# Neighbourhood attention: keys loaded once and doubled on GpSimd, shorter pattern loads, heads asked for a head earlier

## The chip, the cores and the metric

The kernel runs on one core of a Trainium2 chip. The metric is the device time of one execution in microseconds (us), as the median of several runs. A core has five instruction streams that matter here: TensorE (PE in the profile; PEld is its weight load), VectorE (DVE), ScalarE (ACT), GpSimd (POOL) and SyncE (SP), which issues most of the DMAs. Each engine works through its own stream in order and waits on semaphores for the others. A DMA runs on its own once it is issued.

## The reference

The reference is a network of two layers on 2048 tokens (a grid of 32 rows and 64 columns) and 256 context tokens, width 1024, in 32-bit floats. Layer 0 is a convolution beside full attention; layer 1 is Fourier mixing beside neighbourhood attention; each ends with a gate and an output projection. The change lies in the neighbourhood attention of layer 1, which has 8 heads of 64 channels:

```python
s_win = einsum('brqhd,brkwhd->bhrqkw', qg, kb) * scale + bias      # 8 rows of the grid around a query's row
s_win = where(col_ok, s_win, NEG_INF)                              # 16 columns around a query's column
s_ctx = einsum('brqhd,bchd->bhrqc', qg, kc) * scale                # and all 256 context tokens
p = softmax(concatenate([s_win, s_ctx]))
o = p_win @ v_window + p_ctx @ v_context
```

The bias depends on the offset between query and key, and on the head.

## The kernel before

A product of 32-bit floats is made from two rounded parts, a high and a low one (`a = 0, 1` in the code): a query's high part stands on partitions 0 to 63 and its low part on 64 to 127, and one product with 128 rows of contraction takes both against the same key part. For that the key part must stand **twice**, on partitions 0 to 63 and again on 64 to 127. `load_keys` (L1511) therefore loads each of a head's two key tiles (`nk0`, `nk1`, 128 x 2304) by two DMAs of 64 x 2304 from the same place in memory, and the queries (`nq`, 128 x 2048) by two of 64 x 2048. The tiles of a head come from `kp[h % 2]`, two pools of one buffer each: a head's keys can be loaded once the scores of the head two before it are done.

The bias and the mask are kept as patterns: for each head, nine kinds of [128 x 512], loaded as three tiles `pat0`, `pat1`, `pat2` of [128 x 3 x 768] whose first 256 columns (the context) are zero.

The work of a head is cut into four **units** (t = 0 to 3, 16 columns of the grid each), and a unit's scores into four **chunks** (i = 0 to 3, a band of rows). A chunk is this chain over the engines:

- TensorE: four products into one PSUM tile `ns`, two over the 256 context keys (L1577, a = 0 and 1), two over the window's 384 or 512 keys (L1581).
- DVE: `evict` (L1589) adds the pattern and takes the least value; later a reciprocal of the sum (L1603).
- ACT: the exponential (L1596).
- POOL: `normalise` (L1604), [128 x 640] or [128 x 768].

When a unit's four chunks are normalised, six jobs follow it: transposes on TensorE (`npt`, L1635), the split into high and low on ACT (`nhi`, L1640) and DVE (`nlo`, L1642), and products with the values (`nav`, L1655 and L1656). After the last, ACT copies the sum to `ny2`, a DMA moves half of it to other partitions (`ny3`, L1670), and POOL adds the two into the output `yd` (L1673). Values come by `load_values` (L1540): four DMAs of `nv` for each unit (L1549), one of `nvc` for each head (L1544).

What sets the order: `stream` (L1734) writes the order of TensorE, DVE, ACT and POOL by hand. It goes through the units (i = 0 to 31) and their six jobs (j = 0 to 5); the scores run two units and two chunks ahead of the jobs. In each step `extra(i, j)` may add work of its own. SyncE's order is not written out: a scheduler places its DMAs by what they wait for, except those of the first units that are put into the program's order by `keep_in_program_order`. SyncE works through its queue in order, with eight places for DMAs in flight; a DMA that finds its place taken, or its buffer not free, holds all behind it.

Just ahead of the stage the Fourier mixing ends: its last transforms (L1406 to L1408, L1456 to L1458) are on TensorE, its last results are stored by DMAs from ACT's queue (L1477, four of 1 MB).

Of the kernel before, what the change touches and what calls it, by code (L numbers as in the profile page):

```python
# [20 lines left out]
P = 128  # L21
# [28 lines left out]
def dft_tables():  # L50
    """Cosines and sines of 512 rows for the even and the odd frequencies, and those of a channel group."""
# [9 lines left out]
class Stream:  # L61
    """What is due on each engine in the coming steps."""
# [21 lines left out]
class Build:  # L84
# [132 lines left out]
    def adaln(self, layer, j, raw, psum, mo, brow=None):  # L217
        """256 columns of the shift, scale and gate of one layer: in four steps.

        Four column tiles hold sums over a quarter of the rows each, for both conditions.  # L220
        """
# [161 lines left out]
    def load_w(self, raw_of, wp, w, n0, scale=1.0, eng=None, hold=None, load=True):  # L383
        """High and low parts of 256 columns of a weight, as two halves of its rows."""
# [22 lines left out]
    def mm_channel(self, ps, w, h, c, cols, ks=range(KT)):  # L407
        """ps[128 channels, tokens] from weight columns c*128.. and a block's columns."""
# [25 lines left out]
    def ab_proj(self):  # L434
# [5 lines left out]
        with ExitStack() as es:  # L440
# [134 lines left out]
            def ada_tiles():  # L575
                """Where the modulation's weights wait, 256 columns at a time: in tiles that nothing else needs yet."""
# [191 lines left out]
    def load_kv(self):  # L768
        """Keys as [high; high] and as [low; four rows of ones], and values."""
# [19 lines left out]
    def ab_attention(self):  # L789
        """Scores with the keys on partitions, shifted by each query's greatest score.  # L790

        A unit is two heads of one group for 256 queries. Its greatest scores come from products of one pass, with
        the queries on partitions, a unit ahead; they are rounded and go into the scores as four more rows of the
        contraction, one for each 128 queries.
        """
        nc = self.nc
        with ExitStack() as es:
# [56 lines left out]
            def chunk(i, qt, c):  # L854
                """Part of the least (negated) score of 128 queries."""
# [54 lines left out]
            def add(i, k):  # L910
                """Sums over the keys: one on DVE, one on Pool."""
# [32 lines left out]
            def total(i):  # L944
                """A row of sums, which DMAs put on 128 partitions for the reciprocals, and copy to all for the products."""
# [123 lines left out]
    def load_wout_part(self, raw, w, k, n, eng):  # L1069
        """One block of the rows of half of an output projection's columns."""  # L1070
        ins = self.nc.sync.dma_start(raw, w[k * P : (k + 1) * P, n * 512 : n * 512 + 512])
        if n == 0:
            self.tc.keep_in_program_order(ins)
        yield 1
        hi, lo = self.wout[2 * n : 2 * n + 2]
        self.split(hi[:, k], lo[:, k], raw, eng)
# [15 lines left out]
    def out_norm(self, psum, b):  # L1092
        """Layer norm and SiLU of the convolution of 256 tokens."""
# [58 lines left out]
    def out_gate(self, b):  # L1152
        """Gates 256 tokens of both branches and splits them."""
# [182 lines left out]
    # Rows n and 2048-n, then n and 1024-n, are folded together, so that 512 rows are left for the even and for  # L1336
    # the odd frequencies of the cosine and of the sine part; row 512 is added as a vector of signs.
    def fourier_early(self, psum):
        """What is ready before the last input projections are: channel tables, a table, the first two groups."""
# [24 lines left out]
    def fold(self, g, gp, psum):  # L1364
        """A group's folded rows after the channel transform, with rows on partitions."""
# [48 lines left out]
    def dft_table(self, q, rp):  # L1414
        """A quarter of the table of the sequence transform, split."""
# [458 lines left out]
```

## Time and profile before

| what | value |
|---|---|
| median of 3 runs (lowest, highest) | 2954.23 us (2945.24, 2960.78) |
| span of the profiled execution, first to last instruction | 2944.6 us |
| what the median lies above that span | 9.6 us |
| mean granted TensorE clock | 0.970 |
| busy: PE, DVE, POOL, ACT | 94%, 63%, 52%, 39% |
| the stage of the change | 2405 to 2758 us of the span |
| moved by DMA from 2405 to 2745 us | 77.89 MB, 229 GB/s |

The page lists no time of its own for the profiled execution, only its span, so the span stands for it. PE's busy share is an average over the whole program: in most of it the large projections and the attention of layer 0 keep TensorE busy. Busy times of a stage are read in windows of that stage. "Clock" is the share of full speed that was granted to TensorE; it falls for some microseconds after TensorE was idle. A row "X <- Y" among the waits says that X was idle until Y was done.

### The profile page before, as it was taken

Reading aid. Unit: us, or ns where it says so; the run is one execution under the profiler, and the core shown is the slowest. Engines: PE = TensorE matmul, PEld = TensorE weight load, DVE = VectorE, ACT = ScalarE, POOL = GpSimd, SP = SyncE. Lnnn points to the kernel's source line nnn. Section 1 sums busy time; section 2 is a strip of 40 time slices with the busy share of each in tenths; the row PEclk is TensorE's granted clock in tenths of the full one; section 3 lists DMA queues with packets and bytes.
Section 4 is the critical chain, followed back from the end, with each engine's and each line's share of the span. In section 5 each row is a group of like instructions: output and inputs, shape, how many; then the busy total and the mean of one; then the engine's idle time right before and its main releaser. Section 6 shows DMA issues by size and latency. Waiting matters only on the chain.

```text
span 2944.6 us, 40977 instructions
## 1 busy us (share of the span) xinstructions
PE 2764.9 (94%) x14481; PEld 2128.3 (72%) x14481; DVE 1855.9 (63%) x2867; ACT 1134.3 (39%) x2103; POOL 1531.5 (52%) x1173
## 2 busy tenths in 40 slices
PE   7988799986999999999999999999999997998998
PEld 5988799886444444444445887988898886888787
DVE  4798869896877788888887564101211336777663
ACT  3223131320354555555554223123222335777421
POOL 3568624846465788778785754222122312455343
PEclk9999899998999999999999999999999998999999
DMA  8224131361642343331123653433333349999852
GB/s 249 91 77 147 53 106 47 96 179 36 196 136 78 123 138 101 90 121 55 51 63 106 235 166 136 150 127 106 126 140 128 111 152 238 220 246 225 273 197 89
DMA packets 345752, 397.66 MB, mean 135 GB/s; under 512 B 54844, under 2 KB 270444, under 8 KB 340555
## 3 DMA queue, kind: packets, MB, share of 16 engines
q1 hardware_dynamic: 344971, 390.85, 44.9%
q10 hardware_dynamic: 576, 4.19, 0.4%
q8 instruction: 114, 1.87, 0.3%
q14 instruction: 91, 0.75, 0.1%
HBM read 270.34 MB, written 129.78 MB: 136 GB/s over the span
## 4 chain that ended last, share of the span: by engine, by line
PE 65%; DMA 11%; DVE 9%; POOL 6%; issue 4%; ACT 1%; SPq 0%; POOLq 0%; ACTq 0%; DVEq 0%
PE av L900 9%; PE s L885 9%; PE mm L415 7%; PE mm L417 7%; PE mm L416 7%; PE m L862 6%; DVE acc L517 5%; DMA nv<-v_d 4%; POOL wlo L431 4%; PE mo L1087 3%; PE mo L1086 3%; PE mo L1085 3%; DMA nk<-k 3%; PE mm L424 2%; PE mm L426 1%
## 5 line engine op out<-in xcount | busy, mean ns | idle before, releaser
L431 POOL TENSOR_TENSOR wlo<-wraw,whi 128x1024 fp32r<-128x1024 f32 x86 | 323.8, 3774 | 499.7 <-ACT whi L430 481.1
L864 DVE TENSOR_REDUCE ast<-m 128x1 f32<-128x512 f32 (+1 forms) x656 | 398.7, 626 | 176.8 <-PE m L862 174.5
L890 ACT ACTIVATE pr<-s 128x512 f32<-128x512 f32 x584 | 343.1, 595 | 298.6 <-PE s L885 253.9
L925 POOL TENSOR_TENSOR accp<-accp,pr 128x512 f32<-128x512 f32 x283 | 398.7, 1409 | 88.1 <-ACT pr L890 74.2
L517 DVE SCALAR_TENSOR_TENSOR acc<-u,cw,acc 128x1151 f32<-128x1151 f32 (+1 forms) x240 | 366.5, 1582 | 0.0
L900 PE MATMUL av<-pr,vt 128*64 128x512 f32 x1168 | 317.4, 622 | 0.0
L417 PE MATMUL mm<-hi_ab,wlo 128*128 128x384 f32 x768 | 260.6, 341 | 39.1 <-POOL wlo L431 39.1
L415 PE MATMUL mm<-hi_ab,whi 128*128 128x384 f32 x768 | 261.0, 346 | 11.6 <-DVE qraw L729 7.2
L416 PE MATMUL mm<-lo_ab,whi 128*128 128x384 f32 x768 | 261.7, 342 | 0.0
L415 PE MATMUL mm<-hi_cd,whi 128*128 128x512 f32 x640 | 250.8, 392 | 1.1 <-ACT hi_cd L379 1.1
L416 PE MATMUL mm<-lo_cd,whi 128*128 128x512 f32 x640 | 250.1, 391 | 0.4 <-DVE lo_cd L380 0.4
L417 PE MATMUL mm<-hi_cd,wlo 128*128 128x512 f32 x640 | 246.7, 390 | 0.0
L417 PEld LDWEIGHTS mm<-hi_ab,wlo 128*128 128x128 f32 x768 | 147.5, 192 | 39.8 <-POOL wlo L431 39.8
L925 DVE TENSOR_TENSOR accd<-accd,pr 128x512 f32<-128x512 f32 x165 | 165.7, 1004 | 0.9 <-ACT pr L890 0.5
L1642 DVE TENSOR_TENSOR nlo<-npt,nhi 128x512 fp32r<-128x512 f32 x192 | 123.6, 644 | 62.1 <-ACT nhi L1640 61.4
L862 PEld LDWEIGHTS m<-k1h,q 128*128 128x128 f32 x328 | 62.2, 190 | 132.9 <-DVE ast L864 84.9
L415 PEld LDWEIGHTS mm<-hi_ab,whi 128*128 128x128 f32 x768 | 147.5, 193 | 14.1 <-DVE qraw L729 7.6
L1604 POOL TENSOR_SCALAR npr<-npr,nst 128x640 f32<-128x640 f32 (+1 forms) x128 | 108.1, 858 | 89.8 <-DVE nst L1603 66.7
L371 DVE TENSOR_SCALAR ht<-ptr,scale,shift 128x384 f32<-128x384 f32 (+2 forms) x96 | 61.2, 671 | 147.4 <-PE ptr L368 146.7
L862 PEld LDWEIGHTS m<-k0h,q 128*128 128x128 f32 x328 | 63.3, 195 | 125.0 <-DVE ast L864 80.6
L430 ACT ACTIVATE whi<-wraw 128x1024 fp32r<-128x1024 f32 x88 | 92.9, 1059 | 148.3 <-PE mm L416 135.5
L416 PEld LDWEIGHTS mm<-lo_ab,whi 128*128 128x128 f32 x768 | 147.8, 193 | 0.8 <-DVE lo_ab L380 0.8
(321 smaller groups left out, 7002.1 us busy)
## 6 DMA issues: line engine op xcount, KB each, us to landing
wraw<-in_cd_w_in_dram SPq DMA_DIRECT2D x46, 512.0 KB, 4.0
wraw<-in_ab_w_in_dram SPq DMA_DIRECT2D x42, 512.0 KB, 3.5
pat_d<-big SPq DMA_DIRECT2D x72, 256.0 KB, 3.7
nk<-k SPq DMA_DIRECT2D x32, 576.0 KB, 12.7
pat<-pat_d SPq DMA_DIRECT2D x24, 768.0 KB, 6.5
nv<-v_d SPq DMA_DIRECT2D x128, 128.0 KB, 7.0
adaraw<-in_ab_w_ada_dram SPq DMA_DIRECT2D x24, 512.0 KB, 6.1
adaraw<-in_cd_w_ada_dram SPq DMA_DIRECT2D x24, 512.0 KB, 3.7
```

What stands on the lines that cost most here:

```text
L415: nc.tensor.matmul(ps, a, hh[:, k, cols], start=k == 0, stop=False)
L416: nc.tensor.matmul(ps, a, hl[:, k, cols], start=False, stop=False)
L417: nc.tensor.matmul(ps, b, hh[:, k, cols], start=False, stop=k == KT - 1)
L431: (eng or nc.vector).tensor_tensor(out=lo, in0=src, in1=hi.bitcast(F32), op=ALU.subtract)
L517: ins = nc.vector.scalar_tensor_tensor(out=acc[:, :n], in0=u[:, tap : tap + n], scalar=cw[:, ch, tap : tap + 1], in1=acc[:, :n], op0=ALU.m ...
L862: nc.tensor.matmul(ps[:, :n], lhs, kt[hp // 2][0][:, a : a + n], start=True, stop=True)
L864: nc.vector.tensor_reduce(out=s["st"][:, qt, col : col + 1], in_=ps[:, :n], axis=AX.X, op=ALU.min)
L885: nc.tensor.matmul(ps[:], kt[hp // 2][key][:, k * P : k * P + P], s[x][:].rearrange("p j n -> p (j n)"), start=key == 0, stop=key == 1,)
L890: nc.scalar.activation(pr[:], ps[:], AF.Exp, scale=-1.0)
L900: nc.tensor.matmul(s["av"][x * 64 : x * 64 + 64], vt[:, k - 1 + x, kv * 64 : kv * 64 + 64], s["pr"][k - 1 + x][:], start=k == 1, stop=k == ...
L925: eng.tensor_tensor(out=s[name][:], in0=first_in[:], in1=s["pr"][k][:], op=ALU.add)
L1642: return lambda: nc.vector.tensor_tensor(out=lo[:, :o], in0=pt[:, :o], in1=hi[:, :o].bitcast(F32), op=ALU.subtract)
```

## The change

Four things, all in `natten`:

- For heads 1 to 7 each key tile is loaded once, to partitions 0 to 63; GpSimd then copies it to 64 to 127 in six pieces of 384 columns (`double`), twelve for a head. Head 0 is loaded twice as before (`whole`).
- The copies for head h + 1 are issued one in each step while the jobs of head h's units 0 and 1 run (`extra`).
- A pattern tile is loaded by two DMAs, one of [128 x 2 x 384] for the first and the last kind, one of [128 x 512] for the middle one, so that the columns 384 to 511 of the first and last kind, which no chunk reads, are left out.
- The keys and queries of head h + 1 are asked for where those of head h were asked for (of head 1: one unit later), four units ahead. Only head 0's are put into the program's order.

```diff
+            def load_head(h, whole):
+                m, r0 = h // 2, (h % 2) * 64
+                qt = kp[h % 2].tile([P, S], F32R, name="nq", tag="nq")
+                ks = [kp[h % 2].tile([P, T], F32R, name=f"nk{a}", tag=f"nk{a}") for a in range(2)]
+                heads[h] = (qt, ks)
+                for a in range(2):
+                    load(whole, ks[a][0:64].bitcast(F32), self.k2_d[m][a, r0 : r0 + 64])
+                    if whole:
+                        load(whole, ks[a][64:128].bitcast(F32), self.k2_d[m][a, r0 : r0 + 64])
+                for a in range(2):
+                    load(whole, qt[64 * a : 64 * a + 64].bitcast(F32), self.q2_d[m][a, r0 : r0 + 64])
+
+            PIECE = T // 6
+
+            def double(h, x):
+                a, i = divmod(x, 6)
+                k = heads[h][1][a]
+                cols = slice(i * PIECE, i * PIECE + PIECE)
+                nc.gpsimd.tensor_copy(k[64:128, cols], k[0:64, cols])
...
             def load_keys(u):
                 h, t = u
                 first = u in units[:5]
...
-                if t == 0:
-                    qt = kp[h % 2].tile([P, S], F32R, name="nq", tag="nq")
-                    load(qt[0:64].bitcast(F32), self.q2_d[m][0, r0 : r0 + 64])
-                    load(qt[64:128].bitcast(F32), self.q2_d[m][1, r0 : r0 + 64])
-                    ks = []
-                    for a in range(2):
-                        k = kp[h % 2].tile([P, T], F32R, name=f"nk{a}", tag=f"nk{a}")
-                        for r in range(2):
-                            load(k[r * 64 : r * 64 + 64].bitcast(F32), self.k2_d[m][a, r0 : r0 + 64])
-                        ks.append(k)
-                    heads[h] = (qt, ks)
+                if u == units[0]:
+                    load_head(0, True)
                 if t != 2:
                     kind = kind_of[t]
-                    load(
-                        pats[kind][:, :, 256:768],
-                        self.pat_d[:, h].rearrange("(r k) p c -> k p r c", k=3)[kind],
-                    )
+                    pat = self.pat_d[:, h].rearrange("(r k) p c -> k p r c", k=3)[kind]
+                    load(first, pats[kind][:, ::2, 256:640], pat[:, ::2, 0:384])
+                    load(first, pats[kind][:, 1, 256:768], pat[:, 1])
+                if t == (h == 0) and h + 1 < HEADS:
+                    load_head(h + 1, False)
...
+                if i % 4 < 2 and i // 4 + 1 < HEADS:
+                    double(i // 4 + 1, 6 * (i % 4) + j)
```

The order of TensorE, DVE and ACT stays as it was, row by row. SyncE's queue and POOL's change; three places show how. The first is SyncE at the start of the stage. Before, from the first load on (`nk0_21811`, `nk1_21814` and `nq_21808` are head 0's, `nvc_22294` is head 1's):

```order
L1544 DMA nvc_22294<-v2_d_120 128x2x128 [waits DMAHW0_49,DVE_49]
L1517 DMA nq_21808<-q2_0_112 64x2048 [waits DMAHW2_49,PE_49]
L1517 DMA nq_21808<-q2_0_112 64x2048 [waits DMAHW3_49]
L1517 DMA nk0_21811<-k2_0_116 64x2304 [waits DMAHW4_49,PE_49]
L1517 DMA nk0_21811<-k2_0_116 64x2304 [waits DMAHW5_49]
L1517 DMA nk1_21814<-k2_0_116 64x2304 [waits DVE_49,DMAHW6_49,PE_49,Pool_49]
L1517 DMA nk1_21814<-k2_0_116 64x2304 [waits DMAHW7_49]
L1517 DMA pat0_21800<-pat_d_132 128x3x512 [waits DMAHW0_49,PE_49]
```

And with the change (`nk0_21822`, `nk1_21823` and `nq_21821` are head 1's, `nk0_21809`, `nk1_21810` and `nq_21808` head 0's):

```order
L1513 DMA nk0_21822<-k2_0_116 64x2304 [waits DMAHW0_49,DVE_49,DMAHW4_49,PE_49,Pool_49]
L1513 DMA nk1_21823<-k2_0_116 64x2304
L1513 DMA nq_21821<-q2_0_112 64x2048 [waits DMAHW2_49]
L1513 DMA nq_21821<-q2_0_112 64x2048 [waits DMAHW3_49]
L1556 DMA nvc_22316<-v2_d_120 128x2x128
L1513 DMA nk0_21809<-k2_0_116 64x2304 [waits DMAHW6_49]
L1513 DMA nk0_21809<-k2_0_116 64x2304 [waits DMAHW7_49]
L1513 DMA nk1_21810<-k2_0_116 64x2304 [waits DMAHW0_49,DVE_49]
L1513 DMA nk1_21810<-k2_0_116 64x2304 [waits DMAHW1_49]
L1513 DMA nq_21808<-q2_0_112 64x2048 [waits DMAHW2_49]
L1513 DMA nq_21808<-q2_0_112 64x2048 [waits DMAHW3_49]
L1513 DMA pat0_21800<-pat_d_132 128x2x384 [waits DMAHW4_49,PE_49]
```

Head 1's loads now stand ahead of head 0's, and the first of them carries the wait on PE, DVE and POOL that stood at head 0's second key. (Before, head 1's stood behind the patterns and the first values.) For the later heads the key loads keep their place between values and patterns, two rows less.

The second place is POOL at the border between two heads, here ahead of head 2. Before, the last unit of head 1:

```order
L1673 TENSOR_TENSOR yd_22151<-ny2_22408,ny3_22409 64x32x16 [waits DMAHW5_49]
L1604 TENSOR_SCALAR npr_22510<-npr_22510,nst_22516 128x640 [waits PE_49,DVE_49,Activation_49,Pool_49]
L1604 TENSOR_SCALAR npr_22534<-npr_22534,nst_22540 128x768 [waits PE_49,DVE_49,Activation_49,Pool_49]
L1604 TENSOR_SCALAR npr_22574<-npr_22574,nst_22580 128x768 [waits DVE_49,PE_49,Activation_49]
L1604 TENSOR_SCALAR npr_22599<-npr_22599,nst_22605 128x640 [waits PE_49,DVE_49,Activation_49,Pool_49]
```

With the change, the same five rows (`nk1_22006` is head 2's; its copies are those numbered 6 to 11):

```order
L1537 COPY nk1_22006<-nk1_22006 64x384 [waits DMAHW1_49,DMAHW5_49,DMAHW0_49,Pool_49]
L1537 COPY nk1_22006<-nk1_22006 64x384
L1685 TENSOR_TENSOR yd_22171<-ny2_22431,ny3_22432 64x32x16 [waits DMAHW0_49]
L1616 TENSOR_SCALAR npr_22535<-npr_22535,nst_22541 128x640 [waits PE_49,DVE_49,Activation_49,Pool_49]
L1537 COPY nk1_22006<-nk1_22006 64x384 [waits Pool_49]
L1616 TENSOR_SCALAR npr_22560<-npr_22560,nst_22566 128x768 [waits PE_49,DVE_49,Activation_49,Pool_49]
L1537 COPY nk1_22006<-nk1_22006 64x384 [waits Pool_49]
L1537 COPY nk1_22006<-nk1_22006 64x384
L1616 TENSOR_SCALAR npr_22602<-npr_22602,nst_22608 128x768 [waits PE_49,DVE_49,Activation_49,Pool_49]
L1537 COPY nk1_22006<-nk1_22006 64x384 [waits Pool_49]
L1616 TENSOR_SCALAR npr_22628<-npr_22628,nst_22634 128x640 [waits PE_49,DVE_49,Activation_49,Pool_49]
```

Six copies stand among that unit's normalisations, behind the addition; six more among those of the unit ahead.

The third place is TensorE at the first chunk of head 2, with the change:

```order
L1589 MATMUL ns_22671<-nk0_22005,nq_22004 128x256 [waits DVE_49,DMAHW7_49,PE_49,Pool_49]
L1589 MATMUL ns_22671<-nk1_22006,nq_22004 128x256 [waits Pool_49]
L1593 MATMUL ns_22671<-nk0_22005,nq_22004 128x384
L1593 MATMUL ns_22671<-nk1_22006,nq_22004 128x384 [waits Pool_49]
L1667 MATMUL nav_22609<-nhi_22557,nv_22318 128x256
```

The rows and their order are those of before, but three of the four products now wait for POOL; the last reads columns that copies 6 to 8 write. Behind them stand the products of an older unit with its values.

More of the change, by code (lines that the diff above doesn't have):

```diff
@@ L1510, in natten, with load @@
             heads, vals, ctxs, probs, youts, left = {}, {}, {}, {}, {}, {}
+            def load(first, dst, src):
+                ins = nc.sync.dma_start(dst, src)
+                if first:
+                    self.tc.keep_in_program_order(ins)
+            def load_head(h, whole):
[15 more added lines that the diff above has]
+                nc.gpsimd.tensor_copy(k[64:128, cols], k[0:64, cols])
             def load_keys(u):
@@ L1514, in load_keys @@
                 first = u in units[:5]
-                def load(dst, src):
-                    ins = nc.sync.dma_start(dst, src)
-                    if first:
-                        self.tc.keep_in_program_order(ins)
-                m, r0 = h // 2, (h % 2) * 64
-                if t == 0:
-                    qt = kp[h % 2].tile([P, S], F32R, name="nq", tag="nq")
-                    load(qt[0:64].bitcast(F32), self.q2_d[m][0, r0 : r0 + 64])
-                    load(qt[64:128].bitcast(F32), self.q2_d[m][1, r0 : r0 + 64])
-                    ks = []
-                    for a in range(2):
-                        k = kp[h % 2].tile([P, T], F32R, name=f"nk{a}", tag=f"nk{a}")
-                        for r in range(2):
-                            load(k[r * 64 : r * 64 + 64].bitcast(F32), self.k2_d[m][a, r0 : r0 + 64])
-                        ks.append(k)
-                    heads[h] = (qt, ks)
+                if u == units[0]:
+                    load_head(0, True)
                 if t != 2:
                     kind = kind_of[t]
-                    load(
-                        pats[kind][:, :, 256:768],
-                        self.pat_d[:, h].rearrange("(r k) p c -> k p r c", k=3)[kind],
-                    )
+                    pat = self.pat_d[:, h].rearrange("(r k) p c -> k p r c", k=3)[kind]
[3 more added lines that the diff above has]
+                    load_head(h + 1, False)
             def load_values(u):
```

## The prediction

> **What bounds the kernel now.** I read the page first (its opening line, the chain, the DMA issues), then a table of windows over the neighbourhood attention, then the waits of that stage, and at last the timelines of TensorE, GpSimd and SyncE around the places that the change touches. The change lies in one stage, so the shares of the whole span only say where to look:
>
> ```profile
> span 2944.6 us, 40977 instructions
> ...
> PE 65%; DMA 11%; DVE 9%; POOL 6%; issue 4%; ACT 1%; SPq 0%; POOLq 0%; ACTq 0%; DVEq 0%
> ...
> nk<-k SPq DMA_DIRECT2D x32, 576.0 KB, 12.7
> pat<-pat_d SPq DMA_DIRECT2D x24, 768.0 KB, 6.5
> nv<-v_d SPq DMA_DIRECT2D x128, 128.0 KB, 7.0
> ```
>
> The three issue rows are all of this stage: 18.9 MB of keys, 18.9 MB of patterns, 16.8 MB of values. Windows of the stage (columns: length, busy time of PE, PEld, DVE, ACT, POOL with counts, granted clock, DMA share, GB/s):
>
> ```profile
> 2412.00:2440.00 28.00, 27.21 (x142) 23.02 (x141) 9.23 (x18) 6.75 (x14) 4.68 (x5) 1.00 0.87 233
> 2440.00:2470.00 30.00, 19.66 (x111) 14.34 (x111) 21.25 (x58) 19.15 (x41) 11.90 (x14) 0.89 1.06 255
> ...
> 2440.00:2710.00 270.00, 230.17 (x1553) 211.07 (x1554) 198.20 (x502) 192.39 (x411) 123.29 (x135) 0.91 1.05 237
> 2710.00:2740.00 30.00, 29.26 (x219) 27.11 (x218) 26.30 (x67) 27.26 (x60) 17.22 (x20) 1.00 0.58 172
> ```
>
> For 270 us the DMA engines are full (share 1.05 at 237 GB/s) while TensorE is not and runs at clock 0.91. Once the last loads are done, TensorE is full at clock 1.00. So two limits lie close together: transfers until 2710, TensorE after. The waits of the stage (total, times, longest) and the gaps name the transfers:
>
> ```profile
> PE nav L1655 <- DMA nv<-v_d: 25.5, 6, 7.6
> PE ns L1577 <- DMA nk<-k: 8.9, 2, 4.5
> ...
> 2449.40 0.38 PE L1635 MATMUL npt<-ident,npr 128*128 128x128 f32 x2
> ...
> 2465.51 0.55 PE L1577 MATMUL ns<-nk,nq 128*128 128x256 f32 x1 [4.32 <-DMA nk<-k]
> ...
> 2514.37 0.48 PE L1577 MATMUL ns<-nk,nq 128*128 128x256 f32 x2
> ...
> 2691.82 0.35 PE L1655 MATMUL nav<-nhi,nv 128*128 128x256 f32 x1 [2.57 <-DMA nv<-v_d]
> ...
> 2703.02 0.48 PE L1577 MATMUL ns<-nk,nq 128*128 128x256 f32 x2
> ...
> 2731.78 0.48 PE L1577 MATMUL ns<-nk,nq 128*128 128x256 f32 x2
> ```
>
> 2449.40 is the first transpose of the loop; 2514.37 and 2703.02 are the first scores of heads 2 and 7, five heads apart, so a head takes 37.7 us; 2731.78 is the last chunk of scores. GpSimd shows what a unit takes when nothing is late:
>
> ```profile
> 2700.58 1.69 POOL L1604 TENSOR_SCALAR npr<-npr,nst 128x768 f32<-128x768 f32 x2 [1.30 <-DVE nst L1603]
> 2702.35 1.29 POOL L1673 TENSOR_TENSOR yd<-ny,ny 64x512 f32<-64x512 f32 x1
> 2704.22 1.68 POOL L1604 TENSOR_SCALAR npr<-npr,nst 128x640 f32<-128x640 f32 x2 [0.59 <-DVE nst L1603]
> 2708.35 1.69 POOL L1604 TENSOR_SCALAR npr<-npr,nst 128x768 f32<-128x768 f32 x2 [2.44 <-DVE nst L1603]
> 2710.12 1.29 POOL L1673 TENSOR_TENSOR yd<-ny,ny 64x512 f32<-64x512 f32 x1
> 2712.01 1.69 POOL L1604 TENSOR_SCALAR npr<-npr,nst 128x640 f32<-128x640 f32 x2 [0.59 <-DVE nst L1603]
> ```
>
> The same pair of normalisations comes 7.79 us later, so a head needs 31.2 us where nothing stalls, 6.5 less than it takes. From 2449.40 to 2731.78 are 282.4 us for the 118 chunks that follow the first ten, 29.5 units; 29.5 x 7.79 = 229.8. **Stalls cost 52.6 us in this stage**, in gaps and in what comes behind them, shown at one gap by three windows:
>
> ```profile
> 2689.25:2691.80 2.55, 0.00 (x1) 0.01 (x1) 1.91 (x5) 1.12 (x3) 1.85 (x2) 1.00 1.06 248
> 2691.80:2695.50 3.70, 3.68 (x18) 3.70 (x19) 0.76 (x2) 0.66 (x2) 2.75 (x4) 0.54 1.17 229
> 2695.50:2703.00 7.50, 7.50 (x58) 7.09 (x57) 6.16 (x15) 6.87 (x15) 5.31 (x6) 1.00 1.14 240
> ```
>
> An idle 2.55 us is followed by 3.7 us at clock 0.54, in which about 3.7 x 0.46 = 1.7 us of work is lost.
>
> **The change part by part. Bytes.** Heads 1 to 7 load two key pieces of 576 KB instead of four, and three patterns of 640 KB instead of 768: 1536 KB less a head, 1.57 MB; at 237 GB/s that is 6.6 us, so a head's transfers fall from 37.7 to about 31.1 us, just TensorE's 31.2. The values that were late in the gaps stand in the queue behind the key loads, and now behind two of them less (2 x 2.5 us at the same rate), which is about the size of the mean gap (25.5 / 6 = 4.3). I book the whole 52.6 as gained, and set against it 2 us (0 to 12) for values that are still late, since the two limits now are equal. Splitting each pattern adds 24 SyncE issues of some 0.5 us; SyncE is not waited for, nothing.
>
> **The start.** This is where order shows a loss. In the kernel before, head 0's keys went first; the rows and the wait of SyncE there:
>
> ```profile
> 2410.73 1.22 SPq L1517 DMA_DIRECT2D nq<-q  x2
> 2412.03 15.66 SPq L1517 DMA_DIRECT2D nk<-k  x4
> 2430.48 8.66 SPq L1517 DMA_DIRECT2D pat<-pat_d  x3
> ...
> SPq L1517 <- PE pg L1408: 10.9, 2, 10.3
> ...
> 2424.08 3.61 SPq L1517 DMA_DIRECT2D nk<-k  x2
> ...
> 2440.81 0.81 DVE L1589 CUSTOM_DVE_ANT_0 npr<-ns,pat 128x640 f32<-128x640 f32 x1
> ...
> 2431.12 0.33 ACTq L1477 DMA_DIRECT2D yc<-yf  x1
> 2442.98 0.33 ACTq L1477 DMA_DIRECT2D yc<-yf  x1
> ```
>
> Queries and the first half of the keys went out from 2410.7; the last two key loads waited for the Fourier stage's matmul L1408 until 2424.08; the first eviction came at 2440.81, when the Fourier stage had ended on TensorE too. Now head 1's keys stand first and carry that wait (head 0's second key, which had it, shows no wait on PE any more, so the one ahead covers it). All of head 1 and of head 0 therefore starts at 2424.08, or at the latest at 2430.48, where the pattern waits on PE in both. From there to the first pattern go 2176 KB (head 1), 128 KB, 3328 KB (head 0, still whole), 640 KB: 6.4 MB, and two stores of 1 MB each of the Fourier result, which were issued at 2431 and 2443 on another queue: 8.5 MB. At 233 to 255 GB/s (the first two windows above) that is 33.4 to 36.5 us: first eviction near 2459, **18.5 us later**. Bounds: 16 (the stores out of the way) and 25 (start at 2430.48). TensorE is idle for all of it, and by the row above starts at half clock: 2 us. The 8.9 us for head 1's keys are gone with it, but they lie in the 52.6 already.
>
> **The copies.** 84 of them, [64 x 384], on GpSimd. No row shows such a copy; the nearest are
>
> ```profile
> L1604 POOL TENSOR_SCALAR npr<-npr,nst 128x768 f32<-128x768 f32 x64 | 57.9, 908 | 62.7 <-DVE nst L1603 41.4 <-ACT nhi L1640 16.3 <-ACT wout L430 2.6
> L1604 POOL TENSOR_SCALAR npr<-npr,nst 128x640 f32<-128x640 f32 x64 | 51.8, 809 | 27.0 <-DVE nst L1603 25.3 <-PE npt L1635 0.7 <-ACT npr L1596 0.2
> ```
>
> From 640 to 768 columns adds 0.10 us, so 384 columns would be 0.60 on that line and 0.49 in proportion to 640. A copy does less than a product of two factors; I take 0.5, with 0.35 and 1.0 as bounds (half of the 640 row with its fixed part gone; twice my value). [...]
>
> Twelve copies are 6 us in the two units ahead of a head. GpSimd's idle time there is 2 x (2.44 + 0.59) = 6.1 us, so the sum fits, but not the order. Copy 8 (counted from 0) must be done before the second window product of the head's first chunk, and by the order it stands behind the normalisation of the chunk four back. That one is ready late: at head 7 the pair begins at 2704.22, and its first half ends at 2705.03, 2.0 us after the chunk's own start at 2703.02. So even a copy at no cost makes TensorE wait: the product is due some 0.6 us after the start, and gets its keys 2.0 after it. The copies ahead push further: replaying the rows with 0.5 us a copy and 0.1 between (the gap between neighbours in the rows), with copy 5 between them the two normalisations from 2700.58 on end at 2703.1, copies 6 and 7 run to 2704.2, the addition (1.29) to 2705.5, the normalisation to 2706.3, copy 8 to 2706.9: the product waits from 2703.6, **3.3 us**. Chunks 1 and 2 wait 0.1 to 0.3 more for copies 9 and 11. With 0.35 us it is 2.4, with 0.7 some 5, with 1.0 some 8. Behind such a gap comes the half clock, 1.5 us. So 5 us a head, at seven heads **35 us**; at the bounds 7 x 2.4 = 17 and 7 x 9.5 = 67. In TensorE's written order the products and transposes of older units are queued behind the waiting product, so nothing else fills the gap.
>
> [...]
>
> **Four units ahead.** In the queue the key loads of heads 2 to 7 stand where they stood, between the same values and patterns; what decides is when the buffer of the head before comes free. I book nothing.
>
> **Sum.** -52.6 + 2 + 18.5 + 2 + 35 = +5 us: the span goes from 2944.6 to about 2949. The profile's span lies 9.6 us under the median of the three runs (2954.23), which I carry over: **2959 us**. What the change wins on the transfers, it gives back at its start and at the heads' borders. For this kernel 0.5% is 14.8 us.
>
> **The rivals.**
> *A, the copies hide.* If a copy takes 0.35 us, or GpSimd runs ahead more than in the rows because DVE and ACT are less held up, the border costs 2.4 us and little clock: 17 us instead of 35, and with a start of 16: -52.6 + 2 + 16 + 2 + 17 = -16; without late values and without the clock's share at the borders (2 us each, 14) it is -21: about 2936. For it: GpSimd is busy only 17.22 of 30 us in the undisturbed window. Against it: the 2.0 us by which the normalisation comes after the chunk's start does not depend on the copy's price.
> *B, GpSimd becomes the bound at the borders.* From a copy price of about 0.7 us on, the twelve (8.4 us) no longer fit the 6.1 us of idle time, and each border costs 5 us and 2.5 of clock: 7 x 7.5 = 52; with 1.0 us 67. -52.6 + 2 + 18.5 + 2 + 52 to 67 = +22 to +37, slower: about 2983. For it: the normalisations and additions are in the same queue, and what is late there is late for the transposes. Against it: the rows at 640 columns.
> *C, it is not loaded ahead, and the values stay late.* The key loads keep their place in the queue, and each border keeps a wait of 2 to 4 us for values, beside that for the copies: 7 x 3 = 21 on top of my sum: about 2980, slower. For it: transfers and TensorE now take the same 31 us a head. Against it: with 5 us of copy waits a head lasts 36 us, and the transfers have 5 us of slack.
>
> **How the numbers follow.** My forecast 0.44, A 0.26, B 0.20, C 0.10. Faster is A and nothing else: 0.26. Slower are B and C: 0.30. Same 0.44: the forecast's own range is 2945 to 2970. For eight in ten I go from A's 2934 to B's 2988, with some of the ends left out.
>
> **What would show it.** Right: a first eviction near 2459 with TensorE idle before it; DMA share under 1 in the middle of the stage; no TensorE wait for values over 3 us, and instead seven waits of ns for the GpSimd copy line, 3 to 4 us each, with clock 0.5 behind; a head of 36 us. Wrong: a copy row far from 500 ns; a first eviction near 2441 (the start is then free, and the change some 18 us faster than I say); or borders without a wait, which would make A right. If the values still wait by 4 us, C holds.

## The result, and the profile after

The changed kernel takes **2974.03 us** (median), the kernel before 2956.34 us in the same runs: a ratio of 1.0062 with a 95% interval of 1.0048 to 1.0077, so some 18 us slower. The likeliest case of the prediction was no change that can be told (2959 us, from 2945 to 2970). The time lies above that, on the slower side, to which the prediction had given 0.30; it is still inside the wide range for eight in ten, which runs from about 2934 to 2988.

The page after, its opening line and the DMA issues that answer to those of before:

```profile
span 2980.6 us, 41109 instructions
...
nv<-v_d SPq DMA_DIRECT2D x128, 128.0 KB, 3.0
...
nk<-k SPq DMA_DIRECT2D x18, 576.0 KB, 6.5
```

Keys now land in 6.5 us instead of 12.7, values in 3.0 instead of 7.0. The transfers are relieved, as the windows of the stage show too (columns as in the prediction: length, busy time and count of five engines, clock, DMA share, GB/s). The first row is most of the stage, the next two are one head:

```profile
2480.00:2750.00 270.00, 235.18 (x1497) 217.38 (x1496) 186.88 (x464) 182.10 (x386) 157.22 (x208) 0.87 0.71 173
...
2522.00:2541.00 19.00, 14.26 (x71) 12.87 (x70) 8.92 (x22) 8.29 (x19) 9.39 (x13) 0.73 0.93 204
2541.00:2563.80 22.80, 22.80 (x172) 21.53 (x171) 20.74 (x53) 20.67 (x45) 15.69 (x21) 1.00 0.52 144
```

The DMA engines went from a share of 1.05 to 0.71, and yet TensorE gets no more done: in 270 us it is busy for 235 instead of 230, but its clock fell from 0.91 to 0.87. Within a head it is full at full clock from 2541.00 on, and all that is lost is lost in the 19 us ahead of that. The waits of the stage name the two places, the start and the borders between heads:

```profile
PEld ns L1593 <- POOL nk L1537: 36.6, 14, 3.2
PE ns L1593 <- POOL nk L1537: 32.3, 14, 2.9
...
PE ns L1589 <- DMA nq<-q: 16.2, 1, 16.2
```

(PEld is the weight load ahead of the same product; the two rows are one set of 14 waits, two at each of seven borders.) No wait of TensorE for values is left; before, it was 25.5 us.

To set the stage apart from the rest, this table takes each profile from the last product of the Fourier stage to the first product of the last chunk of scores. "First unit" is the time from a head's first chunk to its fifth, for heads 2 to 7; 7.8 us is the pace without stalls.

| kernel | ratio to before (95%) | stage, us | first unit, us |
|---|---|---|---|
| before, two profiles | | 293.6, 303.8 | 7.8 (the third unit of heads 2 to 6 is the slow one: 10.6 to 18.6) |
| the change, two profiles | 1.0062 (1.0048 to 1.0077) | 324.0, 324.6 | 16.9 to 17.9 |
| before with the shorter patterns alone | 0.9977 (0.9964 to 0.9990) | 292.5 | 7.8 |
| E1: the change, head 0 first | 1.0007 (0.9987 to 1.0027) | 313.7 | 17.0 to 18.1 |
| E2: the change, copies of heads 2 to 7 a unit earlier | 0.9900 (0.9880 to 0.9919) | 271.5 | 7.8 to 8.2 |
| E3: the change, copies in unit 0 alone | 0.9897 (0.9873 to 0.9921) | 266.5 | 7.8 to 11.9 |
| E4: the change, copies 9 to 11 a unit earlier | 1.0002 (0.9988 to 1.0016) | 299.5 | 13.7 to 14.3 |
| E1 and E2 | 0.9864 (0.9845 to 0.9883) | 264.2 | 7.8 |
| E1 and E3 | 0.9885 (0.9863 to 0.9906) | 260.3 | 7.8 to 12.0 |
| E1 and E2, head 1's copies in unit 0, ny3 on ACT's queue | 0.9968 (0.9954 to 0.9981) | 283.4 | 7.8 to 8.8 (others up to 14.0) |
| E1 and E3, ny3 on ACT's queue | 0.9965 (0.9952 to 0.9978) | 287.0 | 7.8 to 10.1 (others up to 13.8) |
| E1 and E3, output stored in halves | 0.9870 (0.9850 to 0.9890) | 257.5 | 7.8 to 9.7 |

### The profile page after: what moved, and what is told of

It is laid out like the page before. It is cut to its first block, busy times and chain, and to the rows that moved or that the text cites. A ratio compares the mean times of both kernels' runs of the same rounds, so it can differ in the third digit from the quotient of the medians.

```text
span 2980.6 us, 41109 instructions
## 1 busy us (share of the span) xinstructions
PE 2787.6 (94%) x14481; PEld 2144.8 (72%) x14481; DVE 1861.0 (62%) x2867; ACT 1135.8 (38%) x2103; POOL 1578.9 (53%) x1257
## 5 line engine op out<-in xcount | busy, mean ns | idle before, releaser
L415 PEld LDWEIGHTS mm<-hi_ab,whi 128*128 128x128 f32 x768 | 146.7, 192 | 12.7 <-DVE qraw L729 6.2
```

The source lines that it names most:

```text
L415: nc.tensor.matmul(ps, a, hh[:, k, cols], start=k == 0, stop=False)
```

## A border in the trace

The change's border at head 2, on three engines (GpSimd, then TensorE, then DVE; start, duration, and in brackets the idle time ahead and what ended it):

```profile
2522.66 0.95 POOL L1537 CAST nk<-nk 64x384 fp32r<-64x384 f32 x2
2523.69 1.27 POOL L1685 TENSOR_TENSOR yd<-ny,ny 64x512 f32<-64x512 f32 x1
2524.95 0.79 POOL L1616 TENSOR_SCALAR npr<-npr,nst 128x640 f32<-128x640 f32 x1
2525.80 0.50 POOL L1537 CAST nk<-nk 64x384 fp32r<-64x384 f32 x1
...
2533.26 0.90 POOL L1616 TENSOR_SCALAR npr<-npr,nst 128x768 f32<-128x768 f32 x1 [4.95 <-DVE nst L1615]
2534.22 0.50 POOL L1537 CAST nk<-nk 64x384 fp32r<-64x384 f32 x1
```

```profile
2526.35 0.69 PE L1593 MATMUL ns<-nk,nq 128*128 128x384 f32 x1 [2.58 <-POOL nk L1537]
...
2530.57 1.50 PE L1647 MATMUL npt<-ident,npr 128*128 128x128 f32 x6
2531.72 0.77 PE L1589 MATMUL ns<-nk,nq 128*128 128x256 f32 x2
2532.30 0.46 PE L1593 MATMUL ns<-nk,nq 128*128 128x512 f32 x1
2534.78 0.51 PE L1593 MATMUL ns<-nk,nq 128*128 128x512 f32 x1 [2.02 <-POOL nk L1537]
```

```profile
2532.57 0.42 DVE L1654 TENSOR_TENSOR nlo<-npt,nhi 128x256 fp32r<-128x256 f32 x1 [1.54 <-ACT nhi L1652]
2532.91 0.15 DVE L1615 RECIPROCAL nst<-nst 128x1 f32<-128x1 f32 x1
```

The first wait is the one foreseen: copies 6 and 7, the addition, a normalisation, copy 8 at 2525.80, and at 2526.35 the product that reads it, 2.58 us late. The second was not. Follow it backwards: the third chunk's product at 2534.78 waits for copy 11 (2534.22), which stands behind a normalisation (2533.26); GpSimd had been idle 4.95 us for that one's reciprocal (2532.91); DVE has the reciprocal behind the split `nlo` (2532.57), though the sum that it reads had been ready since 2524.55; the high part of that split ACT makes from six transposes that TensorE ran at 2530.57, **right ahead of the chunk that then waits**. (ACT, too, had first waited for TensorE's products with the values, until 2530.86, and comes to the split at 2532.16.) TensorE waits for a chain that begins with its own work two rows earlier and runs once around ACT, DVE and GpSimd. And after its idle 2.58 us the clock was 0.50 (from 2526.35 to 2532.00, without a break), and those transposes took 1.50 us, where in the kernel before six took 0.84 us at clock 1.00.

## The experiments

Two theories stood against each other: that the copies cost by their **place** in GpSimd's order, or by their **work** there. And the start was either a loss of its own or one that the transfers would have taken anyway.

**E2: copies of heads 2 to 7 a unit earlier.** Head 1's stay in place, as a control.

```diff
-                if i % 4 < 2 and i // 4 + 1 < HEADS:
-                    double(i // 4 + 1, 6 * (i % 4) + j)
+                if i < 2:
+                    double(1, 6 * i + j)
+                if i % 4 in (3, 0) and 2 <= (i + 5) // 4 < HEADS:
+                    double((i + 5) // 4, 6 * ((i + 1) % 4) + j)
```

> Edit: the changed kernel with the GpSimd copies of heads 2 to 7 issued one unit (six steps) earlier; head 1's stay where they are, as a control within the run. In the changed kernel the first unit of each of heads 1 to 7 takes 17.8 us instead of 7.8, with two TensorE waits on copies (2.6 and 2.0 us) and two stretches of half clock. Theory (place): TensorE waits because copies 8 and 11 stand behind normalisations that only come late, whatever a copy costs. Then at heads 2 to 7 both waits and the half clock go, 6 x 10 = 60 us, head 1's first unit keeps 17.8 us, and some of it (up to 10 us) comes back as waits for values, since transfers and TensorE then need about 31 us a head each: 2915 to 2925 us. Rival (GpSimd's work): the 0.5 us copies overload GpSimd wherever they stand; the normalisations of the earlier unit are late instead, transposes wait for them, and the time stays at 2965 to 2974.

Measured: 2930.46 us, 0.9900 (0.9880 to 0.9919). TensorE's waits on the copies:

```profile
PE ns L1593 <- POOL nk L1537: 4.2, 2, 2.9
```

And a window over heads 2 to 7:

```profile
2500.00:2700.00 200.00, 195.69 (x1434) 183.88 (x1432) 176.71 (x445) 172.29 (x369) 150.28 (x196) 0.98 0.97 212
```

Only head 1's two waits are left, of the 14. The six other borders run at the pace, the same copies at the same cost on the same engine: place, not work. The stage is 52.5 us shorter. Waits for values, which were expected to come back, did not, though the DMA share is 0.97; what remains is two slow units, of 13.7 and 9.5 us, in which GpSimd itself comes late (below). The time, 2930, lies a little above the 2915 to 2925 expected.

**E1: head 0 first.** Head 1's loads go into the program's order, behind the patterns.

```diff
-                if t == (h == 0) and h + 1 < HEADS:
+                if t == 3 * (h == 0) and h + 1 < HEADS:
                     load_head(h + 1, False)
...
-                    load(whole, ks[a][0:64].bitcast(F32), self.k2_d[m][a, r0 : r0 + 64])
+                    load(h < 2, ks[a][0:64].bitcast(F32), self.k2_d[m][a, r0 : r0 + 64])
...
-                    load(whole, qt[64 * a : 64 * a + 64].bitcast(F32), self.q2_d[m][a, r0 : r0 + 64])
+                    load(h < 2, qt[64 * a : 64 * a + 64].bitcast(F32), self.q2_d[m][a, r0 : r0 + 64])
```

> Edit: the changed kernel with head 1's keys and queries put into the program's order behind head 0's keys and the three patterns; all else as in the change. Theory: 16 us of the loss are TensorE standing idle at the start (first score at 2459.1 where the Fourier stage ended at 2442.5), because head 1's loads go first and carry a wait. Then the first score follows the Fourier stage within 3 us, 3 us come back because the first values now stand behind head 1's keys, and the time falls by 10 to 14 us to about 2962; borders unchanged at 17.8 us. Rival: the stage is limited by the bytes it must move, so an earlier start is given back before head 2: 2970 to 2974.

Measured: 2965.12 us, 1.0007 (0.9987 to 1.0027), so about 0.55% less than the change. The first score comes 0.2 us after the Fourier stage instead of 16.6. Of these 16.4 us the stage keeps 10.3: the first units take 6.8, 7.5 and 6.4 us instead of 5.1, 3.9 and 5.3. Two rows of ACT show what holds them up:

```profile
2449.58 0.33 ACTq L1477 DMA_DIRECT2D yc<-yf  x1
2449.94 1.28 ACT L1608 ACT_TABLE_LOAD   x1 [8.49 <-DMA pat<-pat_d]
```

ACT has one more store of the Fourier result to issue, and stands idle 8.49 us until a pattern load of SyncE's has landed. Its first exponential comes at 2451.23, 7.5 us after the first eviction (2443.69); in the kernel before it came 3.8 us after (2444.63 and 2440.81). The borders are as in the change. The loss at the start is real and lies in the order of the loads, but only some 10 us of it are to be had this way.

**E1 and E2 together.**

> Edit: the two edits together (copies of heads 2 to 7 a unit earlier, head 0 loaded first). If start and borders are separate losses, the gains add: 60 + 12 less up to 12 of value waits, 2900 to 2915 us. If the transfers become the bound once TensorE no longer waits, the two gains overlap, values are late at the borders as in the kernel before, and it stays above 2920.

Measured: 2920.61 us, 0.9864 (0.9845 to 0.9883). Expected were 2900 to 2915, so the gains add only in part: 52.5 and 10.3 us apart, 59.8 together in the stage. At one of the two slow units left beside head 1's border, GpSimd and SyncE show this:

```profile
2624.69 0.95 POOL L1537 CAST nk<-nk 64x384 fp32r<-64x384 f32 x2
2634.80 1.29 POOL L1685 TENSOR_TENSOR yd<-ny,ny 64x512 f32<-64x512 f32 x1 [9.16 <-DMA yd<-yd]
...
2627.98 0.34 SPq L1690 DMA_DIRECT2D yd<-yd  x1
```

The addition is the first of a new pair of heads. It waits for the 1 MB store of the pair before, as `yd` has one buffer, and for its own small DMA (`ny3`), issued behind that store at 2631.60; when it comes, 9.16 us later, everything on GpSimd is late.

**Only the shorter patterns**, on the kernel before.

```diff
-                    load(
-                        pats[kind][:, :, 256:768],
-                        self.pat_d[:, h].rearrange("(r k) p c -> k p r c", k=3)[kind],
-                    )
+                    pat = self.pat_d[:, h].rearrange("(r k) p c -> k p r c", k=3)[kind]
+                    load(pats[kind][:, ::2, 256:640], pat[:, ::2, 0:384])
+                    load(pats[kind][:, 1, 256:768], pat[:, 1])
```

> Edit: the kernel before with only the shorter pattern loads (two DMAs, 640 KB instead of 768 KB). 3 x 128 KB a head at 237 GB/s are 1.66 us a head. Theory (the stage of the kernel before is bound by transfers from 2440 to 2710): every byte counts, 7 x 1.66 = 12 us off, up to 18 with the half clock behind shorter gaps: 2938 to 2945 us. Rival (only the key loads, which stand right ahead of the late values, matter): under 4 us, 2953 to 2957.

Measured: 2952.56 us, 0.9977 (0.9964 to 0.9990): 6.8 us less, between the two expectations. TensorE still waits for values:

```profile
PE nav L1654 <- DMA nv<-v_d: 26.4, 6, 6.8
```

That is as much as before (25.5). So the bytes left out of the patterns gave back about half of their transfer time (6.8 of 12 us), and the values stayed late. That in the change they are in time points to the key loads ahead of them; no run halves the key loads alone.

**E3: the copies squeezed into unit 0**, two in each step, for heads 1 to 7.

```diff
-                if i % 4 < 2 and i // 4 + 1 < HEADS:
-                    double(i // 4 + 1, 6 * (i % 4) + j)
+                if i % 4 == 0 and i // 4 + 1 < HEADS:
+                    double(i // 4 + 1, 2 * j)
+                    double(i // 4 + 1, 2 * j + 1)
```

> Edit: the changed kernel with the same twelve copies a head, but two in each step of unit 0 alone, so that copy 8 stands a unit ahead of its first reader and GpSimd has 6 us of copies in a unit with 3 us of idle time. Theory (place): the normalisations of that unit are some 3 us late, nothing reads them for a unit, so every border is 7.8 us, head 1's too: 7 x 10 = 70 us less in the stage than the change, with the waits for GpSimd's other late work that the run with the earlier copies showed (about 8 us) left: 2920 to 2930. Rival (GpSimd's work): the squeezed unit makes transposes wait on normalisations, 3 us and half clock a head: 2945 to 2960.

Measured: 2924.69 us, 0.9897 (0.9873 to 0.9921), as place would have it (2920 to 2930). GpSimd in such a unit:

```profile
2504.74 1.86 POOL L1537 CAST nk<-nk 64x384 fp32r<-64x384 f32 x4
2506.68 1.30 POOL L1685 TENSOR_TENSOR yd<-ny,ny 64x512 f32<-64x512 f32 x1
2507.96 0.79 POOL L1616 TENSOR_SCALAR npr<-npr,nst 128x640 f32<-128x640 f32 x1
...
2516.86 3.48 POOL L1616 TENSOR_SCALAR npr<-npr,nst 128x640 f32<-128x640 f32 x4
```

It is busy without a break and falls behind, and then does four normalisations in a row from 2516.86 and has caught up; TensorE does not stop. Six microseconds of work in a unit with three to spare cost nothing here, where the normalisations are not read for another unit. But not every border is at the pace: in the first chunk of heads 4 and 6 TensorE still waits 1.7 us on a copy, and those units take 11.9 and 10.9 us. There the copies came late because GpSimd did, idle ahead of an addition for 9.82 us at one and 7.06 us at the other. The first of the two:

```profile
2569.12 1.29 POOL L1685 TENSOR_TENSOR yd<-ny,ny 64x512 f32<-64x512 f32 x1 [9.82 <-DMA yd<-yd]
```

**E4: the last three copies alone a unit earlier.** This tests the second wait by itself: copies 0 to 8 stay.

```diff
-                if i % 4 < 2 and i // 4 + 1 < HEADS:
+                if i // 4 + 1 < HEADS and (i % 4 == 0 or i % 4 == 1 and j < 3):
                     double(i // 4 + 1, 6 * (i % 4) + j)
+                    if i % 4 == 0 and j >= 3:
+                        double(i // 4 + 1, 6 + j)
```

> Edit: the changed kernel with only copies 9 to 11 of each head moved, a unit earlier, doubling up with copies 3 to 5; copies 0 to 8 stay in their places. In the change the first chunk waits 2.6 us (copy 8) and the third 2.0 us (copy 11). Theory (a loop over the engines makes the second wait: copy 11 stands behind a normalisation whose reciprocal stands behind a split of transposes that TensorE runs right ahead of the waiting product): the first wait stays at 2.6 to 3.5 us, the second goes, with one stretch of half clock of 3.4 to 6.8 us left: a head's first unit 12 to 14 us instead of 17.8, 7 x 4 to 6 = 28 to 42 us off: 2932 to 2946. Rival (GpSimd is simply late after the first wait, by the copies' work and the half clock): TensorE still waits about 2 us later in the unit, on a normalisation instead of a copy: 2960 to 2974.

Measured: 2960.71 us, 1.0002 (0.9988 to 1.0016). The time missed the expected 2932 to 2946 and lies at the lower end of what the rival gave (2960 to 2974). The waits decide between the two. The rival needs a wait of TensorE later in the unit, on a normalisation, and at the seven borders there is none; the waits on the copies and the window of one border are those of the theory:

```profile
PE ns L1593 <- POOL nk L1537: 17.1, 7, 2.7
PE ns L1589 <- POOL nk L1537: 10.9, 7, 3.0
```

```profile
2526.00:2540.00 14.00, 11.28 (x71) 10.51 (x72) 7.65 (x21) 7.27 (x17) 7.52 (x10) 0.88 1.04 220
```

The waits left, on copy 8 (17.1 us) and on copy 6 (10.9), are both in the first chunk, 4.0 us a head; GpSimd is later there by the three copies more. None is left in the third chunk. A head's first unit takes 13.7 to 14.3 us, as the theory had it, and the stage is 24.5 us shorter than the change's. The time fell by 0.6%, some 18 us, where 28 to 42 were expected: the first chunk's wait had been put at 2.6 to 3.5 us, and is 4.0.

**The small DMA on ACT's queue**, to take it out from behind the loads.

```diff
-                nc.sync.dma_start(y3[a], y2[o])
+                nc.scalar.dma_start(y3[a], y2[o])
```

> Edit: both earlier edits, head 1's copies two a step in unit 0, and the 64 x 512 DMA from ny2 to ny3 issued from ACT's queue instead of SyncE's. In the run with both edits three stretches are left over the pace: head 1's border (10.7 us) and two units (4.3 and 7.6 us), where GpSimd's addition waits for that DMA behind the 1 MB store of yd and other loads in SyncE's queue (9.16 us at one) and everything behind it is late. Theory: on a queue of its own the DMA lands in 2 to 3 us, the two units fall to 7.8, head 1's border by about 5: 17 us less, 2900 to 2908 us. Rival: the transfers are the limit there, not the queue, and the wait moves to values or patterns: 2915 to 2921.

> Edit: head 0 loaded first, two copies a step in unit 0 of each head (heads 1 to 7), ny3 from ACT's queue. If place alone counts, this is as fast as the same with copies spread over an earlier pair of units: 2898 to 2908. If GpSimd's work counts, it is 20 us or more slower than that.

Measured: 2945.82 us (0.9968, 0.9954 to 0.9981) and 2944.65 us (0.9965, 0.9952 to 0.9978). Both are slower than without the edit, by some 25 us in the medians, and more than 36 us above what was expected of it (2900 to 2908, 2898 to 2908). The waits of TensorE and ACT in the first of the two, and two rows of ACT's timeline:

```profile
PE npt L1647 <- DVE nlo L1654: 31.1, 13, 4.9
...
ACT npr L1608 <- DMA nv<-v_d: 21.9, 4, 6.3
ACT npr L1608 <- DMA pat<-pat_d: 13.7, 3, 5.7
```

```profile
2532.67 0.47 ACTq L1682 DMA_DIRECT2D ny<-ny  x1
2533.19 0.83 ACT L1608 ACTIVATE npr<-npr,nst 128x640 f32<-128x640 f32 x1 [6.30 <-DMA nv<-v_d]
```

What I had read as the wait for `ny3` behind the store was, by its releaser, the wait for the store itself, and one such wait, of 4.3 us, is left with the edit. And the cure was worse: ACT reads neither values nor patterns. It is idle for 6.30 us until some load of SyncE's has landed, then issues its DMA (2532.67) and goes on: the order of both kernels gives DMAs of either queue one of the same eight places (`DMAHW0` to `DMAHW7` in its rows), and the row in ACT's order waits for its place. It is the wait that E1 showed at the start. What stood behind loads in SyncE's queue now holds up ACT's exponentials and splits behind the same loads, and TensorE waits for those instead. Copies in unit 0 or a unit earlier make no difference here either.

**E1 and E3, ny3 left with SyncE.**

> Edit: the changed kernel with head 0 loaded first and two copies a step in unit 0; ny3 stays in SyncE's queue. Theory: the start (head0_first took 10 us off the stage) and the borders (one_unit took 50 us off the time) are separate losses, and what made the two runs with ACT's queue slow is that queue alone (ACT waits up to 6.3 us for a free place for the DMA). Then this is 8 to 12 us below one_unit's 2925: 2912 to 2918, ratio to before about 0.986. Rival: two copies a step is what was slow there; then it stays at 2925 to 2945.

Measured: 2919.77 us, 0.9885 (0.9863 to 0.9906), a little above the 2912 to 2918 expected. It differs from the second of the two slow kernels in the queue alone, so the queue was the cause. Against the same kernel without the edit to the start (0.9897, 0.9873 to 0.9921) the intervals overlap: once the borders are mended, the start's 16 us are worth 6 us in the stage. This and E1 with E2 (2920.61 us) beat the change and the kernel before; which of the two is faster can't be told.

**The output stored in halves**, added to that kernel, to test what makes GpSimd late.

```diff
-                    youts[m] = yp.tile([P, S], F32, name="yd", tag="yd")
+                    youts[m] = youts[0] if youts else yp.tile([P, S], F32, name="yd", tag="yd")
...
-                    if h % 2 == 1 and t == 3:
-                        nc.sync.dma_start(self.yd_d[m][:], y[:])
+                    if t == 3:
+                        nc.sync.dma_start(self.yd_d[m][a], y[a])
```

> Edit: head 0 first and copies in unit 0 (2919.77 us, stage 260.3 us), and the output of two heads stored in two halves, each after its own head, from one tile that is not renewed. There GpSimd's first addition of heads 2 and 4 waits 7.7 and 9.9 us for the store of the two heads before (1 MB), since the tile has one buffer; units of 9.4 to 12.2 us follow. Theory (that store, not the queue in which ny3 stands, is what made GpSimd late in the runs before): these waits go, the units near 12 fall to 7.8 to 8.5, the stage to about 252, the time by 6 to 9 us to 2911 to 2914. Rival (the small ny3 DMA behind the loads in SyncE's queue is late all the same, as in the 7.4 and 5.5 us waits of the same trace): the wait stays under another name, 2917 to 2922.

Measured: 2921.19 us, 0.9870 (0.9850 to 0.9890): the same time. GpSimd's waits in the additions, ahead of this edit and with it, and a window over most of the stage:

```profile
POOL yd L1685 <- DMA yd<-yd: 17.6, 2, 9.9
POOL yd L1685 <- DMA ny<-ny: 12.9, 2, 7.4
```

```profile
POOL yd L1685 <- DMA ny<-ny: 18.4, 6, 7.3
```

```profile
2480.00:2700.00 220.00, 213.12 (x1547) 197.67 (x1545) 190.99 (x479) 187.04 (x401) 158.08 (x207) 0.99 1.00 213
```

The waits for the store are gone, and the units near 12 us with them (the longest behind head 0 is now 11.2), but the additions wait more often for `ny3`, and the stage is only 2.8 us shorter. The time is what the rival gave. The DMA share is 1.00, while TensorE is busy for 213 of 220 us at clock 0.99, so both limits are close here; which of them holds the rest, no run separates.

**Two kernels again**, for a second profile of each.

> The kernel before, unchanged, for a second profile. The two profiles differ by 36 us, the medians by 18: either the profile of before was a lucky one in the stage of the change (293.6 us from the end of the Fourier stage to the last scores), then this one shows about 300 to 310 there; or the rest of the program varies, then the stage is again 293 to 296 and the difference lies ahead of it or behind it.

> The changed kernel, unchanged, for a second profile. The first has 324.0 us in the stage where the two profiles of the kernel before have 293.6 and 303.8, so 20 to 30 us more, while the medians differ by 18. If its stage is as regular as its 17.8 us borders look, this one shows 322 to 326 again, and the spread of the difference is that of the kernel before.

Measured: the stage of the kernel before takes 293.6 and 303.8 us, that of the change 324.0 and 324.6. TensorE's waits for values add up to 25.5 us in the first profile of before; in the second:

```profile
PE nav L1655 <- DMA nv<-v_d: 36.2, 6, 8.9
```

In these two pairs the stage differs by 10 us in the kernel before, where late transfers set the pace, and by 0.6 us in the change, where the written order does. With the mean of two each, the change costs 25.6 us in the stage. The medians differ by 18; the rest of the program varies by some 7 us in these four profiles, and what of the remaining 8 us lies there was not settled.

## Why the prediction was right or wrong

**What bounded the stage: right.** With fewer bytes the transfers stopped being the limit (share 0.71), the waits for values went, and the units between borders run at 7.8 us. So the change does gain the 52.6 us. But they are not all left once the borders are mended: 293.6 - 52.6 would be a stage of 241 us, and the shortest of any run has 257.5, with other waits of some microseconds. Part of the 0.71 was slack that the borders gave; without them the share is 0.97 to 1.00, as the prediction's two equal limits (31.1 and 31.2 us a head) would have it.

**The start: right.** Head 1's first key load went out at 2428.39 in the change, 14.1 us ahead of the Fourier stage's end, as the load that carried the wait did before (2424.08 and 2438.22); the lower of the two bounds held. The first score,

```profile
2459.09 0.77 PE L1589 MATMUL ns<-nk,nq 128*128 128x256 f32 x2 [16.19 <-DMA nq<-q]
```

is 16.6 us after the Fourier stage, instead of 0.2; 18.5 were foreseen, from 16 to 25. (It waits for head 0's queries; the prediction had counted up to the first pattern.) The 2 us for half clock behind it (0.52 from 2459.09 to 2464.32) were not lost: the first twelve chunks take 14.3 us in the change (5.1, 3.9 and 5.3 a unit) and 14.6 before. In the kernel before, DVE was at the Fourier stage's last rows until 2440.81; in the change it is free at once, and from 2464.32 on its rows follow one another almost without a break, so it sets the pace there, not TensorE.

**The copy's price: right**, 0.50 us taken, 0.50 measured:

```profile
L1537 POOL CAST nk<-nk 64x384 fp32r<-64x384 f32 x84 | 40.6, 500 | 3.7
```

**The border: the right mechanism, half the size.** The step that failed is the sentence "Chunks 1 and 2 wait 0.1 to 0.3 more for copies 9 and 11". The first wait was 2.58 us where 3.3 were worked out. But chunk 2 waited another 2.02. The replay had moved GpSimd's rows by their own durations and held the reciprocals at the times of the trace before; the reciprocal ahead of copy 11 was not at a fixed time, it was itself waiting for TensorE, at clock 0.50. So there are two waits, and two stretches of low clock (0.50 from 2526.35 to 2532.00, 0.72 from 2534.80 to 2541.00): of the 19 us at clock 0.73 TensorE is idle for 4.7 (19 - 14.26), and the rest of the loss, some 5 us, is the low clock, where 1.5 were booked. A border costs 10 us, not 5; the seven first units together take 69 us more than the pace, where 35 were foreseen. The run with the last three copies moved shows the second wait to hang on their place. The size of B's loss came about, but not by B's mechanism: the copies took 0.50 us, not 0.7, and in E2 the same copies cost the borders nothing where they were early.

**The clock: right that it falls behind such waits.** The fourteen waits are at most 3.2 us long, and the clock over head 2's border is 0.73. One of the fourteen cost none (see the last section).

**Values that stay late (2 us), and C: wrong, with no harm.** Not one wait for values is left in the change. That the borders give the transfers slack, as the argument against C had it, is not needed for this: in E2, at a share of 0.97, TensorE waits for no values either.

**The sum.** By the first profile of before: -52.6 + 16.4 + 69 = +33, against 30.4 measured in the stage, where +5 was predicted. Of the 26 us between, the borders are 34, less the start's 2, the half clock's 2 and the values' 2; some 2 us are left over, which were not settled. That the time came out only 15 us above the forecast is in part luck: of the 9.6 us by which the median of before lay above its profile, 2.1 lie around the span (a run of 2960.87 us has a span of 2958.8), and the other 7.5 mean that the profiled execution was a short one. They were added to the forecast and hid as much of the border's error.

## What to carry to other kernels

Work that is moved onto an engine with idle time is free only at the right place in its order: ask which instruction stands ahead of it, and follow that one back; if it meets the engine that will wait, the chain is a loop, and here such a loop cost 2.02 us and a stretch of 6.2 us at clock 0.72 at a border, though the new instruction takes 0.5 us. When a wait is replayed from a trace, the waits of the engines beside it move too, and here the clock of 0.50 stretched them (six transposes from 0.84 to 1.50 us). And a scheduler that may place loads freely can put the second thing needed ahead of the first: read the queue, not the program.

## What the runs showed of the hardware

- A wait of 2.02 us was followed by a lowered clock, and one of 2.57 us was not. The stretch from 2534.8 to 2541 behind the first, with no idle time in it, was granted 0.72; the stretch behind the second, which ended at 2608.66 in head 4's first chunk, was granted 1.00:

```profile
2534.80:2541.00 6.20, 6.20 (x33) 5.81 (x34) 3.60 (x8) 3.78 (x8) 2.05 (x2) 0.72 0.77 159
...
2608.66:2612.20 3.54, 3.54 (x26) 3.19 (x26) 2.29 (x4) 1.58 (x3) 1.86 (x3) 1.00 1.03 207
```

- A DMA that ACT issues held ACT until an earlier load of another queue had landed: ACT was idle 6.30 us ahead of one in the stage, and 8.49 us ahead of one at E1's start.
- Loading a key part to 64 partitions and copying it on GpSimd (12 copies, 6.0 us a head) set free two transfers of 576 KB a head. Neither TensorE nor DVE was seen to run slower beside the copies: from 2555.30 to 2563.80 in the change, with six copies in it, TensorE is busy for 8.50 of 8.50 us at clock 1.00, and DVE's split of 128 x 512 takes 690 ns in the change's stage and 689 ns in that of the kernel before.
